# A fifth K pair with seven products in three gate/up chunks of each layer

## The chip, the core and the metric

The kernel runs on one core of a Trainium2 chip. Five engines work side by side, each with an instruction queue of its own: TensorE (PE, matmuls, with PEld for its weight loads), VectorE (DVE), ScalarE (ACT), GpSimd (POOL) and SyncE (SP, which here only issues DMAs). They wait for each other through semaphores. The metric is the device time of one execution in microseconds (us), the median of several.

## The reference

Two layers of a residual trunk over 256 tokens of width 2048, in float32. Each layer has a mixer (two kinds of attention, one input and one output projection) and a SwiGLU block. The change lies in the first half of the latter, the two products `h @ w_gate` and `h @ w_up`:

```python
def swiglu(h, w_gate, w_up, w_down):
    return (jax.nn.silu(h @ w_gate) * (h @ w_up)) @ w_down

for l in range(DEPTH):            # 2 layers
    ...
    h = rms_norm(x, pre_ffn_norm[l])
    f = swiglu(h, w_gate[l], w_up[l], w_down[l])
    x = x + rms_norm(f, post_ffn_norm[l])
```

`w_gate` and `w_up` are 2048 x 5632, `w_down` is 5632 x 2048.

## The kernel before

**Float32 products in three matmuls.** TensorE multiplies in a rounded format. Each operand is therefore split into a high part (ScalarE rounds it, `hi`, `xT[..., 0]`) and a low part (VectorE subtracts, `lo`, `xT[..., 1]`), and `product` (L1033) issues three matmuls: high by high, high by low, low by high (L1036, L1037, L1038). Weights come from memory as float32 tiles of 128 x 2 x 512, 512 KB each, one per K pair (2 x 128 rows of the weight matrix) and 512 columns. `weights_in_turn` holds them in the order in which they are used. `fetch` (L197) issues the loads, `feed` (L276) the splits, four tiles ahead of use (`LOOKAHEAD`).

**The gate/up loop.** The 5632 columns are cut into 11 chunks of 512 (c = 0 to 10), and for each chunk the loop at L1196 runs over 8 K pairs (kp = 0 to 7). A pair has four results to add to: gate and up, each for two halves of the tokens (`banks`, four PSUM banks). Plainly (`eight`, L1169) this takes 2 K halves x 2 token halves x 2 matrices = 8 products, 24 matmuls.

**Seven products.** For some pairs the kernel uses a Strassen-Winograd form (`seven`, L1179, and `seven_products`, L1053): the 2 x 2 blocks (token halves by K halves, and K halves by gate and up) are multiplied with 7 products, 21 matmuls. Four of these add to banks of their own (`extra`: p1, p6, p7, q5), which `shared_part` (L1070) combines once per chunk, after the last such pair. The form needs two more things:

- sums of the weights. `mixed_weights` (L243) makes them for each such pair. The up tile is not loaded alone: `summed` (L233) loads it into a tile `T` from SP's queue, and then POOL's queue (L238) adds the first half of the gate tile to it by an accumulating DMA. The gate tile goes to a tile `G` (L209). VectorE and ScalarE then split G (L286, L289) and T (L259, L260), form T's second half (L267) and G (L268) in place, and split these too (`Th`, `Tl`, L259, L260). There are 4 tiles T, 3 tiles G, 2 tiles each of Th and Tl, and 6 each of the high and low parts of all weights.
- sums of the activations, the `forms`. `pair_sums` (L1162) makes them once per layer and pair, with two sums f (L1166) and `token_sums` (L1040: four combinations, a high part on ScalarE, a low part at L1050). They are kept to the end of the loop, in four places (`sh`, `sl`). `FORM_AT` says before which chunk and position they are made.

Which pairs take seven products is laid down per chunk: pairs 4 and 6 in the first, 4, 5, 6 in the second, and 2, 4, 5, 6 (`SEVEN`) in all others. The other pairs are plain, and their tiles are loaded to `raw` (4 tiles).

**At the end of a chunk** VectorE adds the shared part to the banks and multiplies (L1220 to L1223), ScalarE applies SiLU, and TensorE transposes the result during the next chunk (`flip`). The next chunk adds up in the four banks that this one used as `extra`, and the other way round.

**Rooms.** `late_room` (L346) hands out places of 4 KB per partition, four in turn. In this stage they hold the residual x, which is written to memory in the fourth to seventh chunk (`put_away`), and from the eighth chunk on the activations.

**Order.** The kernel is written as one program. A scheduler orders each engine's queue when the kernel is built: by program order as priority, but by its own estimate of when an instruction can start, so that an instruction whose operands are late is passed by others, on TensorE too. Each queue is then fixed and runs in that order. `issue_after` ties an instruction behind another one: `behind` (L297) puts the next two plain low parts behind the shared part, `after_rests` (L304) puts a form behind the last plain low part, and `not_ahead` (L227) keeps loads of T and G behind a plain load six tiles earlier in the order.

Of the kernel before, what the change touches and what calls it, by code (L numbers as in the profile page):

```python
# [10 lines left out]
F32R = mybir.dt.float32r  # L11
# [6 lines left out]
P = 128  # L18
D = 2048
S = 256  # L20
# [22 lines left out]
SEVEN = (2, 4, 5, 6)  # L43
FIRST_SEVEN = (4, 6)
FIRST_ORDER = (0, 1, 3, 2, 7, 4, 6, 5)
NEXT_SEVEN = (4, 5, 6)
FORM_AT = {(0, 1): 4, (0, 2): 6, (0, 5): 5, (1, 3): 2}
DOWN_SEVEN = ((4, 7, 10, 12, 15, 17, 20), (3, 5, 8, 10, 13, 15, 18))

WARM = 10  # L50
# [10 lines left out]

def gate_sevens(c):

    return (FIRST_SEVEN, NEXT_SEVEN)[c] if c < 2 else SEVEN


# [87 lines left out]
def kernel(  # L154
# [191 lines left out]
    def late_room(shape, name, dtype=F32):  # L346

        return rooms.tile(shape, dtype, tag="late", name=name)
# [691 lines left out]
    def token_sums(pool, spool, bufs, a11, a12, a21, a22, nm, tags=("sh", "sl")):  # L1040

        s = pool.tile([P, 4, P], F32, tag="t2", name=f"s{nm}")
        nc.vector.tensor_tensor(out=s[:, 0, :], in0=a21, in1=a22, op=ALU.add)
        nc.vector.tensor_tensor(out=s[:, 1, :], in0=s[:, 0, :], in1=a11, op=ALU.subtract)
        nc.vector.tensor_tensor(out=s[:, 2, :], in0=a11, in1=a21, op=ALU.subtract)
        nc.vector.tensor_tensor(out=s[:, 3, :], in0=a12, in1=s[:, 1, :], op=ALU.subtract)
        sh = spool.tile([P, 4, P], F32R, tag=tags[0], bufs=bufs, name=f"sh{nm}")
        nc.scalar.activation(sh, s, AF.Copy)
        sl = spool.tile([P, 4, P], F32R, tag=tags[1], bufs=bufs, name=f"sl{nm}")
        nc.vector.tensor_tensor(out=sl, in0=s, in1=sh.bitcast(F32), op=ALU.subtract)  # L1050
        return [(sh[:, j, :], sl[:, j, :]) for j in range(4)]

# [30 lines left out]
    for l in range(L):  # L1083

        pool = Rooms(tc, f"att{l}")
# [12 lines left out]
        forms = {}  # L1098
        for n, (c, kp) in enumerate(plan[l]["order_o"][:16]):
# [5 lines left out]
            if n in (9, 11):  # L1105
                kp = O_SEVEN[(n - 9) // 2]
# [53 lines left out]
        forms = {}  # L1160

        def pair_sums(kp):  # L1162
            f = pool.tile([P, 2, S], F32, tag="t2", name=f"f{l}_{kp}")
            for kk in range(2):
                st = xT[2 * kp + kk]
                nc.vector.tensor_tensor(out=f[:, kk, :], in0=st[:, 0, :].bitcast(F32), in1=st[:, 1, :].bitcast(F32), op=ALU.add)  # L1166
            forms[kp] = token_sums(pool, gu, len(SEVEN), f[:, 0, 0:P], f[:, 1, 0:P], f[:, 0, P:S], f[:, 1, P:S], f"{l}_{kp}")

        def eight(banks, c, kp, toks, first, last):  # L1169
            g, u = weights(plan[l]["gate"][c, kp], LOOKAHEAD), weights(plan[l]["up"][c, kp], LOOKAHEAD)  # L1170
# [225 lines left out]
```

## Time and profile before

| | us |
|---|---|
| median of 3 runs | 2191.11 (2190.64 to 2191.31) |
| profiled execution, its own time | 2191.05 |
| its span, first to last instruction | 2189.4 |
| TensorE busy in the span | 2174.9 |
| VectorE busy | 1901.3 |
| ScalarE busy | 1370.9 |

The profile is of one execution. Its page gives the busy time of each engine, the chain of waits that ended last, and groups of instructions. In rows of instructions, `L289` is a line of the kernel, `lo<-raw,hi` says what is written and what is read, and the bracket at the end of a row in order of time says how long the engine had been idle and what ended that. Busy time of TensorE overlaps between successive matmuls, so distances between starts are used for it here. All times in rows are us from the start of the span, if no ns are given.

### The profile page before, as it was taken

What the parts mean: (1) busy time and instruction counts of PE and PEld (TensorE: products, weight loads), DVE (VectorE), ACT (ScalarE), POOL (GpSimd) and SP (SyncE); (2) the same over time, 40 slices, a digit from 0 to 9 for tenths busy, and PEclk for the clock granted to TensorE, in tenths of its full rate; (3) what the DMA queues carried; (4) which work ended last, traced back from release to release, by engine and by line L of the source; (5) the groups of instructions that cost most, each with busy time, mean ns of one, the idle gap of its engine ahead of it and who ended that gap; (6) DMA issues with size and microseconds to landing.
All of it is one profiled execution on the core that took longest, in us unless ns stands there. A gap on an engine that the chain in (4) does not pass through costs nothing.

```text
span 2189.4 us, 28540 instructions
## 1 busy us (share of the span) xinstructions
PE 2174.9 (99%) x9988; PEld 1791.1 (82%) x9988; DVE 1901.3 (87%) x2610; ACT 1370.9 (63%) x2051; POOL 139.1 (6%) x187
## 2 busy tenths in 40 slices
PE   9999999999999999999999999999999999999998
PEld 7888888888888888888878888888888888888886
DVE  6888658999999999989878886589999999999997
ACT  7666665756656656666665666657665666566664
POOL 1100000010010010000010000000000000100000
PEclk9999999999999999999999999999999999999999
DMA  9545555587687676767464555555867866767683
GB/s 327 189 164 173 192 184 172 180 281 231 219 272 229 198 258 203 247 211 260 147 241 173 177 177 185 193 168 194 277 208 255 256 210 228 238 214 233 207 266 100
DMA packets 138546, 467.28 MB, mean 213 GB/s; under 512 B 15761, under 2 KB 16785, under 8 KB 137889
## 3 DMA queue, kind: packets, MB, share of 16 engines
q1 hardware_dynamic: 122096, 436.29, 57.2%
q0 software_dynamic: 15872, 28.88, 7.5%
q8 instruction: 78, 1.28, 0.2%
q14 instruction: 68, 0.55, 0.1%
q10 hardware_dynamic: 432, 0.28, 0.0%
HBM read 457.00 MB, written 8.39 MB: 213 GB/s over the span
## 4 chain that ended last, share of the span: by engine, by line
PE 95%; DVE 3%; ACT 1%; DMA 0%; issue 0%; DVEq 0%; SPq 0%; ACTq 0%
PE c L1037 10%; PE c L1038 10%; PE c L1036 10%; PE in L1036 7%; PE in L1038 7%; PE in L1037 7%; PE dn L1280 4%; PE dn L1278 4%; PE dn L1277 4%; PE p L1037 3%; PE p L1038 2%; PE p L1036 2%; PE o L536 2%; PE o L537 2%; PE o L538 2%; PE dn L1037 1%
## 5 line engine op out<-in xcount | busy, mean ns | idle before, releaser
L289 DVE TENSOR_TENSOR lo<-raw,hi 128x1024 fp32r<-128x1024 f32 x522 | 625.4, 1219 | 97.6 <-ACT hi L286 96.6
L286 ACT ACTIVATE hi<-raw 128x1024 fp32r<-128x1024 f32 x522 | 540.6, 1055 | 186.0 <-issue 50.3
L1036 PE MATMUL c<-hi,xF 128*128 128x512 f32 x834 | 328.1, 394 | 0.1
L1037 PE MATMUL c<-lo,xF 128*128 128x512 f32 x834 | 325.1, 390 | 0.7 <-DVE lo L289 0.7
L1038 PE MATMUL c<-hi,xF 128*128 128x512 f32 x834 | 324.7, 390 | 0.0
L238 POOL DMA_DIRECT2D T<-in_weights_in_turn_dram x110 | 95.8, 871 | 1679.5 <-PE c L1037 521.3
L1037 PEld LDWEIGHTS c<-lo,xF 128*128 128x128 f32 x834 | 156.7, 188 | 33.4 <-DVE lo L289 2.5
L1038 PEld LDWEIGHTS c<-hi,xF 128*128 128x128 f32 x834 | 156.6, 188 | 32.7
L1036 PEld LDWEIGHTS c<-hi,xF 128*128 128x128 f32 x834 | 156.7, 188 | 31.4 <-ACT xF L455 0.5
L1277 PE MATMUL dn<-hi,jh 128*128 128x512 f32 x432 | 168.3, 389 | 0.0
L1278 PE MATMUL dn<-lo,jh 128*128 128x512 f32 x432 | 168.1, 389 | 0.0
L289 DVE TENSOR_TENSOR lo<-G,hi 128x1024 fp32r<-128x1024 f32 x110 | 134.1, 1219 | 29.7 <-ACT hi L286 29.7
L259 ACT ACTIVATE hi<-T 128x1024 fp32r<-128x1024 f32 x110 | 115.5, 1050 | 40.8 <-PE c L1038 26.5
L259 ACT ACTIVATE Th<-G 128x1024 fp32r<-128x1024 f32 x110 | 116.1, 1055 | 38.1 <-DVE G L268 36.2
L260 DVE TENSOR_TENSOR Tl<-G,Th 128x1024 fp32r<-128x1024 f32 x110 | 134.1, 1219 | 5.3 <-ACT Th L259 5.3
L260 DVE TENSOR_TENSOR lo<-T,hi 128x1024 fp32r<-128x1024 f32 x110 | 134.1, 1219 | 2.6 <-ACT hi L259 2.2
L268 DVE TENSOR_TENSOR G<-G,T 128x1024 f32<-128x1024 f32 x110 | 134.4, 1222 | 2.1
L259 ACT ACTIVATE Th<-T 128x512 fp32r<-128x512 f32 x110 | 68.9, 627 | 104.3 <-DVE T L267 88.3
L1280 PE MATMUL dn<-hi,jl 128*128 128x512 f32 x432 | 132.9, 390 | 0.0
L1036 PE MATMUL in<-hi,xT 128*128 128x512 f32 x328 | 131.9, 404 | 0.5 <-ACT hi L841 0.5
L1036 PE MATMUL in<-hi,xI 128*128 128x512 f32 x328 | 131.1, 401 | 0.0
L1038 PE MATMUL in<-hi,xT 128*128 128x512 f32 x328 | 128.4, 392 | 0.0
(450 smaller groups left out, 4735.6 us busy)
## 6 DMA issues: line engine op xcount, KB each, us to landing
raw<-in_weights_in_turn_dram SPq DMA_DIRECT2D x522, 512.0 KB, 4.6
T<-in_weights_in_turn_dram SPq DMA_DIRECT2D x110, 512.0 KB, 6.3
G<-in_weights_in_turn_dram SPq DMA_DIRECT2D x110, 512.0 KB, 5.8
T<-in_weights_in_turn_dram POOLq DMA_DIRECT2D x110, 256.0 KB, 7.1
GU<-in_weights_in_turn_dram SPq DMA_DIRECT2D x32, 512.0 KB, 6.2
V<-in_weights_in_turn_dram SPq DMA_DIRECT2D x8, 512.0 KB, 4.1
away_ffn<-x SPq DMA_DIRECT2D x8, 512.0 KB, 8.4
xd<-away_ffn SPq DMA_DIRECT2D x8, 512.0 KB, 8.2
```

What stands on the lines that cost most here:

```text
L238: nc.gpsimd.dma_start(sums[i][:, 0, :], stream[i - 1][:, 0, :], accum_op=ALU.add)
L259: nc.scalar.activation(h, w, AF.Copy)
L260: nc.vector.tensor_tensor(out=l, in0=w, in1=h.bitcast(F32), op=ALU.subtract)
L268: nc.vector.tensor_tensor(out=g, in0=g, in1=t2.unsqueeze(1).to_broadcast([P, 2, CW]), op=ALU.add)
L286: nc.scalar.activation(hi, raw, AF.Copy)
L289: rest = nc.vector.tensor_tensor(out=lo, in0=raw, in1=hi.bitcast(F32), op=ALU.subtract)
L1036: nc.tensor.matmul(a, sh, hi, start=first, stop=False, skip_group_check=open_sums[0])
L1037: nc.tensor.matmul(a, sh, lo, start=False, stop=False, skip_group_check=open_sums[0])
L1038: nc.tensor.matmul(a, sl, hi, start=False, stop=last, skip_group_check=open_sums[0])
L1277: nc.tensor.matmul(accs[c, t], sh, hi[:, kk, :], start=first, stop=False, skip_group_check=open_sums[0])
L1278: nc.tensor.matmul(accs[c, t], sh, lo[:, kk, :], start=False, stop=False, skip_group_check=open_sums[0])
L1280: nc.tensor.matmul(accs[c, t], sl, hi[:, kk, :], start=False, stop=last, skip_group_check=open_sums[0])
```

## The change

Pair 3 joins the pairs with seven products in chunks 5, 7 and 9, that is the sixth, eighth and tenth of each layer. Its form is made once per layer in chunk 4, before pair 3 there. The four places for forms are taken, so `token_sums` without a pool takes one late room, which has the size of both its tiles.

```diff
@@ -44,7 +44,9 @@
 NEXT_SEVEN = (4, 5, 6)
-FORM_AT = {(0, 1): 4, (0, 2): 6, (0, 5): 5, (1, 3): 2}
+MORE_SEVEN = (2, 3, 4, 5, 6)
+MORE_AT = (5, 7, 9)
+FORM_AT = {(0, 1): 4, (0, 2): 6, (0, 5): 5, (1, 3): 2, (4, 3): 3}
...
 def gate_sevens(c):
+    if c in MORE_AT:
+        return MORE_SEVEN
     return (FIRST_SEVEN, NEXT_SEVEN)[c] if c < 2 else SEVEN
...
@@ -1044,9 +1048,13 @@
-        sh = spool.tile([P, 4, P], F32R, tag=tags[0], bufs=bufs, name=f"sh{nm}")
+        if spool is None:
+            both = late_room([P, 2, 4, P], f"ss{nm}", F32R)
+            sh, sl = both[:, 0], both[:, 1]
+        else:
+            sh = spool.tile([P, 4, P], F32R, tag=tags[0], bufs=bufs, name=f"sh{nm}")
+            sl = spool.tile([P, 4, P], F32R, tag=tags[1], bufs=bufs, name=f"sl{nm}")
         nc.scalar.activation(sh, s, AF.Copy)
-        sl = spool.tile([P, 4, P], F32R, tag=tags[1], bufs=bufs, name=f"sl{nm}")
         nc.vector.tensor_tensor(out=sl, in0=s, in1=sh.bitcast(F32), op=ALU.subtract)
...
@@ -1164,7 +1172,7 @@
-            forms[kp] = token_sums(pool, gu, len(SEVEN), f[:, 0, 0:P], ...)
+            forms[kp] = token_sums(pool, gu if kp in SEVEN else None, len(SEVEN), f[:, 0, 0:P], ...)
```

More of the change, by code (lines that the diff above doesn't have):

```diff
@@ L1166, in pair_sums @@
                 nc.vector.tensor_tensor(out=f[:, kk, :], in0=st[:, 0, :].bitcast(F32), in1=st[:, 1, :].bitcast(F32), op=ALU.add)
-            forms[kp] = token_sums(pool, gu, len(SEVEN), f[:, 0, 0:P], f[:, 1, 0:P], f[:, 0, P:S], f[:, 1, P:S], f"{l}_{kp}")
+            forms[kp] = token_sums(pool, gu if kp in SEVEN else None, len(SEVEN), f[:, 0, 0:P], f[:, 1, 0:P], f[:, 0, P:S], f[:, 1, P:S], f"{l}_{kp}")
         def eight(banks, c, kp, toks, first, last):
```

## The prediction

> **What bounds the kernel now.** I read the page's busy times first, then the waits of TensorE, then busy times by chunk, then the order in time of TensorE and VectorE in one chunk.
>
> ```profile
> span 2189.4 us, 28540 instructions
> PE 2174.9 (99%) x9988; PEld 1791.1 (82%) x9988; DVE 1901.3 (87%) x2610; ACT 1370.9 (63%) x2051; POOL 139.1 (6%) x187
> ...
> PE p L1037 <- DVE Tl L260: 0.7, 2, 0.5
> ```
>
> TensorE is hardly ever idle: the longest entry for weights is 0.7 us in two waits (who waited; for what; us in all, times, longest). So time falls only if TensorE gets less to do, and rises if VectorE, busy 87% of the span, is late more often. The chunks from the fourth on are alike, so one window tells of them all:
>
> ```profile
> core 0: us, PE busy (x) PEld busy (x) DVE busy (x) ACT busy (x) POOL busy (x), PEclk, DMA share, GB/s
> 621.80:663.60 41.80, 41.80 (x190) 34.60 (x189) 38.99 (x42) 25.35 (x30) 3.46 (x4) 1.00 0.74 241
> ```
>
> The window runs from the start of pair 2 in the sixth chunk to that in the seventh. TensorE is full at full clock, VectorE has 2.8 us of air in 41.8, ScalarE 16. The order in time of TensorE in this window (start, duration, instruction):
>
> ```profile
> 621.84 0.39 PE L1036 MATMUL p<-hi,xF 128*128 128x512 f32 x1
> ...
> 626.60 0.39 PE L1036 MATMUL c<-hi,xF 128*128 128x512 f32 x1
> ...
> 632.04 0.39 PE L1036 MATMUL p<-hi,xF 128*128 128x512 f32 x1
> ...
> 641.56 0.39 PE L1036 MATMUL p<-hi,xF 128*128 128x512 f32 x1
> ...
> 643.83 0.39 PE L1037 MATMUL p<-Tl,sh 128*128 128x512 f32 x1
> ...
> 663.57 0.39 PE L1036 MATMUL p<-hi,xF 128*128 128x512 f32 x1
> ```
>
> Pair 2 with seven products takes 626.60 - 621.84 = 4.76 us for its 21 matmuls, 0.227 each; pair 3 with eight takes 632.04 - 626.60 = 5.44 for 24. A chunk takes 663.57 - 621.84 = 41.73, the window above unrounded.
>
> **The change part by part.** *What it removes.* In three chunks of each of two layers pair 3 goes from eight products to seven: three matmuls, 5.44 - 4.76 = 0.68 us, six times: **-4.08 us**. Transposes and products of other pairs stay.
>
> *What it adds on VectorE.* The kinds in one chunk (count | busy us, mean ns | idle before):
>
> ```profile
> L289 DVE TENSOR_TENSOR lo<-raw,hi 128x1024 fp32r<-128x1024 f32 x8 | 9.6, 1216 | 0.0
> L268 DVE TENSOR_TENSOR G<-G,T 128x1024 f32<-128x1024 f32 x4 | 4.9, 1222 | 0.1
> L289 DVE TENSOR_TENSOR lo<-G,hi 128x1024 fp32r<-128x1024 f32 x4 | 4.9, 1219 | 1.7 <-ACT hi L286 1.7
> L260 DVE TENSOR_TENSOR lo<-T,hi 128x1024 fp32r<-128x1024 f32 x4 | 4.9, 1217 | 0.0
> L260 DVE TENSOR_TENSOR Tl<-G,Th 128x1024 fp32r<-128x1024 f32 x4 | 4.9, 1217 | 0.0
> L267 DVE TENSOR_TENSOR T<-T 128x512 f32<-128x512 f32 x4 | 2.7, 685 | 0.0
> L260 DVE TENSOR_TENSOR Tl<-T,Th 128x512 fp32r<-128x512 f32 x4 | 2.7, 685 | 0.2 <-ACT Th L259 0.2
> L1074 DVE TENSOR_TENSOR w<-p,w 128x512 f32<-128x512 f32 x1 | 0.7, 692 | 0.6 <-PE p L1038 0.6
> ```
>
> A plain pair costs two low parts (L289). A mixed pair costs two low parts as well, and also T (L267), G (L268), and the low parts Tl of T and of G. Successive instructions overlap a little. The order in time of VectorE in the sixth chunk shows it:
>
> ```profile
> 619.53 1.22 DVE L260 TENSOR_TENSOR Tl<-G,Th 128x1024 fp32r<-128x1024 f32 x1
> 622.48 1.23 DVE L289 TENSOR_TENSOR lo<-G,hi 128x1024 fp32r<-128x1024 f32 x1 [1.73 <-ACT hi L286]
> ...
> 624.76 1.22 DVE L289 TENSOR_TENSOR lo<-G,hi 128x1024 fp32r<-128x1024 f32 x1
> ...
> 636.50 1.22 DVE L289 TENSOR_TENSOR lo<-raw,hi 128x1024 fp32r<-128x1024 f32 x1
> 637.64 0.68 DVE L267 TENSOR_TENSOR T<-T 128x512 f32<-128x512 f32 x1
> 638.24 1.22 DVE L289 TENSOR_TENSOR lo<-raw,hi 128x1024 fp32r<-128x1024 f32 x1
> ...
> 641.11 1.21 DVE L289 TENSOR_TENSOR lo<-raw,hi 128x1024 fp32r<-128x1024 f32 x1
> 642.25 1.21 DVE L260 TENSOR_TENSOR Tl<-G,Th 128x1024 fp32r<-128x1024 f32 x1
> ```
>
> The next start follows 1.14 us after that of a 128x1024 subtraction (637.64 - 636.50) and 0.60 after that of a 128x512 one (638.24 - 637.64). So a mixed pair costs 4 x 1.135 + 2 x 0.605 = 5.75 us against 2.27, **3.48 more**, and a changed chunk asks VectorE for 38.99 + 3.48 = 42.5 us while TensorE needs only 41.73 - 0.68 = 41.05. Two chunks together (changed, unchanged) ask 81.5 against 82.8: the debt can be paid, if one chunk may run late into the next.
>
> *Where the debt falls due.* The tightest place is Tl of pair 6: written until 642.25 + 1.21 = 643.46, read at 643.83. Its slack is 0.37 us. In the changed chunk the second half of pair 3's mixing, 3.48 us, comes ahead of this. It can begin when Tl of pair 2 is done (619.53 + 1.22), where VectorE now sits idle 1.73 us until a buffer of high parts comes free. That leaves 3.48 - 1.73 = 1.75 us of delay, and TensorE arrives 0.68 sooner: if all else keeps its order, Tl of pair 6 is 1.75 + 0.68 - 0.37 = **2.06 us late**. The other bound: three subtractions of plain weights (636.50, 638.24, 641.11; 1.13 each), needed only after pair 6, now go ahead of it. With all three behind it, it is 2.06 - 3.40 = 1.34 us early and nothing is lost. The scheduler puts them into gaps between dependent instructions, and their high parts come free as TensorE leaves pairs 4 and 5; I take it that two stay ahead by the new times and one (641.11) goes behind: 2.06 - 1.13 = 0.9 late, or 0.6 when I add up the work from 620.75: 3.48 + 3 x 5.75 + 2 x 1.13 = 23.0, ending 643.75 against 643.15.
>
> Lateness is not all lost, since TensorE's order is laid down with it. The second chunk shows how much. There the same three pairs 4, 5, 6 follow a form (below), and VectorE runs without a pause:
>
> ```profile
> 453.00:480.00 27.00, 26.51 (x117) 21.37 (x116) 26.96 (x34) 17.35 (x20) 1.73 (x2) 1.00 0.69 217
> ...
> 468.75 0.39 PE L1036 MATMUL p<-hi,xF 128*128 128x512 f32 x1
> ...
> 471.76 1.22 DVE L260 TENSOR_TENSOR Tl<-G,Th 128x1024 fp32r<-128x1024 f32 x1
> ...
> 472.16 0.39 PE L1038 MATMUL c<-hi,sl 128*128 128x512 f32 x1
> 473.04 0.50 PE L1037 MATMUL p<-Tl,sh 128*128 128x512 f32 x1 [0.49 <-DVE Tl L260]
> ```
>
> Pair 5 starts at 468.75, and by the order of the sixth chunk (643.83 - 641.56 = 2.27) its Tl would be due at 471.02. It ended at 472.98, 1.96 late. TensorE had taken another product first (472.16), and lost 473.04 - 472.16 - 0.23 = 0.65 us, a third. Of 0.6 to 0.9 late a third is 0.2 to 0.3; pair 5, one pair before, is squeezed too. I take **0.35 us lost in each run of five, 2.1 in all** (bounds 0 and 6 x 2.06 = 12.4).
>
> Behind the waiting matmul nothing but TensorE's own next products is queued. What is late next is the shared part (L1074): it now waits 0.6 us for TensorE, which covers some of the debt, and the next chunk's 1.73 us pause the rest, so the seventh, ninth and eleventh chunks cost nothing; without that cover each lost the remaining 1 us.
>
> *The form of pair 3.* Once per layer in the fifth chunk:
>
> ```profile
> L1166 DVE TENSOR_TENSOR f<-xF x16: 414/418/425, 418.5 to 1547.0; 128x256 f32<-128x256 f32 x16
> L1045 DVE TENSOR_TENSOR s<-f x8: 282/283/293, 419.2 to 1549.3; 128x128 f32<-128x128 f32 x8
> L1050 DVE TENSOR_TENSOR sl<-s,sh x36: 680/684/693, 423.2 to 2138.4; 128x512 fp32r<-128x512 f32 x36
> ```
>
> Two sums, four combinations and a low part (min/median/max ns): with the same overlap of 0.085, 2 x 0.33 + 4 x 0.20 + 0.60 = 2.06 us. The 1.73 us pause falls right behind the place where it is queued, and hides most of it; 0.33 is left against a slack of 0.37. Without that cover 2.06 - 0.37 = 1.7 us are late, and a third of it lost, 0.57. I take less than half of that, 0.25, **0.5 for two layers** (bounds 0 and 2 x 1.7 = 3.4). Its ScalarE copy and those of the mixing (two more per pair, L259) lie in ScalarE's 16 us of air.
>
> *Loads.* Pair 3's two loads become G and T of the same size, with an accumulating load from POOL of half the size on top, six times.
>
> ```profile
> 620.78 0.33 SPq L209 DMA_DIRECT2D G<-in_weights_in_turn_dram  x1
> ...
> T<-in_weights_in_turn_dram SPq DMA_DIRECT2D x110, 512.0 KB, 6.3
> G<-in_weights_in_turn_dram SPq DMA_DIRECT2D x110, 512.0 KB, 5.8
> T<-in_weights_in_turn_dram POOLq DMA_DIRECT2D x110, 256.0 KB, 7.1
> ...
> L286 ACT ACTIVATE hi<-G 128x1024 fp32r<-128x1024 f32 x110 | 115.7, 1052 | 12.0 <-PE c L1038 10.5
> ```
>
> T needs 6.3 + 7.1 = 13.4 us, but four T tiles let pairs 2 to 5 be loaded before the first of them is used, so I take 0. There are only three G tiles: G of pair 5 must wait until Tl of pair 2 is done, the very event that now lets the load at 620.78 go, and lands 5.8 later at 626.6. Its low part runs at 624.76 now and would at about 626.5; with 1.05 us for the high part it can start at 627.6. An order that has other work ready there hides this 1.1 us: cost 0, at most 1.1 per run. The form takes one of the four rooms of x that were put away one chunk earlier, and the later chunks' rooms move on by one, each free long before: 0.
>
> **Sum**, against the profiled execution's own 2191.05 (span 2189.4 and 1.65 around it; the median of the three runs is 0.06 higher): 2191.05 - 4.08 + 2.1 + 0.5 = **2189.6**, -0.07%.
>
> **The rivals.** *All hidden* (2187.0): the order puts all three plain subtractions behind and the form in the pause. For it: 81.5 against 82.8 us for two chunks, and the pause of 1.73. Against it: the 0.37 slack, and the second chunk's loss.
>
> *The order stays* (2200.5, slower): in place Tl of pair 6, the scheduler goes on filling gaps with plain weights as at 636.50 to 641.11, and TensorE stands 2.06 us in each run: 6 x (2.06 - 0.68) = +8.3, and 2 x 0.57 for the form. It decides against the change from 0.68 us a run on, and beyond 0.2% from 1.4. For it: that order in each chunk. Against it: the product taken first at 472.16.
>
> *Three G tiles* (2190.9 to 2197.7, say 2194.3): VectorE idles 1.1 us for pair 5's gate weights, Tl of pair 6 is 0.6 + 1.1 = 1.7 late; with a third of it lost 0.57 a run, with all lost 1.7; and 0.5 for the form. Against it: plain work and T of pair 5 can go first.
>
> *Each changed chunk takes VectorE's time* (2195.5 to 2200.3): if no debt passes to the next chunk, a chunk lasts 42.47, or 43.27 with the 0.6 and 0.2 of idle time that its dependences force (L1074, Tl of T), instead of 41.73: 0.74 to 1.54, six times. Against it: two sets of accumulators let the next chunk's products start before the evacuation ends. The Trainium skill, Perfetto Trace Analysis, "Identifying the Most-Contended Engine", says that for Vector the occupancy is a fair measure of how close it is to its limit and that the engine with the highest occupancy is the one to relieve. By that rule the change loads the wrong engine. The trace agrees that VectorE is near its limit (38.99 of 41.80), not that it sets the time so far.
>
> **How the numbers follow.** The forecast has 0.50, all hidden 0.25, three G tiles 0.10, the order stays 0.09, VectorE's time 0.04, unnamed 0.02. A measurement here can tell about 0.2% from no change, 4.4 us: 2186.7 and 2195.5 are the bounds. All hidden lies 0.3 within the lower bound: a fourth of its chance goes beyond, 0.07 faster with rounding. Slower: 0.09 + 0.04 + 0.03 of three G tiles = 0.16. The rest, 0.77, is the same. The range leaves out these ends: 2186.8 to 2195.0. The forecast's own, with 0 to 0.68 lost a run and 0 to 0.57 a form, is 2187.0 to 2192.2.
>
> **What would show it.** Eighteen matmuls fewer; in the changed chunks a wait of TensorE for Tl (L260) of pair 5 or 6, 0.2 to 0.5 us in all; no idle time of VectorE before pair 4's low part; 41.73 us as before for the unchanged chunks behind them. A wait for Tl over 1.4 us a run, VectorE idle for `hi` of pair 5 behind a G load, or a longer seventh, ninth or eleventh chunk would prove the forecast wrong, and so would time that moves in other stages.

## The result and the profile after

The changed kernel takes 2193.82 us (median of 21 executions, 2192.34 to 2196.9) against 2191.4 of the kernel before (21 executions beside it, 2189.78 to 2192.61): 1.0013 times as long, 95% interval 1.0007 to 1.0019. It is 2.4 us slower. That is less than the 0.2% that was called no change, but the forecast of 2189.6 lay 1.5 us on the faster side. The profiled execution took 2192.96 us.

From the page of the changed kernel, its span, its busy times and the longest entry for weights among TensorE's waits:

```profile
span 2191.3 us, 28616 instructions
...
PE 2175.0 (99%) x9970; PEld 1784.5 (81%) x9970; DVE 1923.6 (88%) x2648; ACT 1380.1 (63%) x2065; POOL 144.4 (7%) x193
...
PE p L1041 <- DVE Tl L264: 1.7, 4, 0.5
```

The eighteen matmuls are gone (9988 to 9970), yet TensorE is busy 2175.0 us as before (2174.9). Its waits for Tl grew by only 1.0 us, from 0.7 to 1.7. So most of what was lost isn't in rows of waits; it shows in the distances between starts. (Lines of the kernel moved by 4 to 8: L1036 to L1038 of before are L1040 to L1042, L260 is L264, L289 is L293, L1074 is L1082.)

The same chunk as in the prediction, first layer, TensorE's starts of pair 2 and pair 6 of the sixth chunk and of pair 2 of the seventh:

```profile
620.96 0.40 PE L1040 MATMUL p<-hi,xF 128*128 128x512 f32 x1
...
640.33 0.39 PE L1040 MATMUL p<-hi,xF 128*128 128x512 f32 x1
...
662.49 0.39 PE L1040 MATMUL p<-hi,xF 128*128 128x512 f32 x1
```

From pair 2 to pair 6 it is 19.37 us, before 641.56 - 621.84 = 19.72; from pair 6 to the next pair 2 it is 22.16, before 22.01. Taken for every chunk, these two distances tell where the time went. Differences to the kernel before, in us, for the first layer and the second:

| from | to | first | second |
|---|---|---|---|
| fifth, pair 6 (the form is made) | sixth, pair 2 | +0.48 | +0.45 |
| sixth, pair 2 | pair 6 (eight to seven products: -0.68) | -0.35 | -0.35 |
| sixth, pair 6 | seventh, pair 2 | +0.15 | +0.12 |
| seventh, pair 2 | pair 6 | +0.25 | +0.23 |
| seventh, pair 6 | eighth, pair 2 | +0.05 | +0.04 |
| eighth, pair 2 | pair 6 (-0.68) | -0.50 | -0.48 |
| eighth, pair 6 | ninth, pair 2 | +0.09 | +0.04 |
| ninth, pair 6 | tenth, pair 2 | +0.66 | +0.66 |
| tenth, pair 2 | pair 6 (-0.68) | -0.64 | -0.66 |
| tenth, pair 6 | eleventh, pair 2 | +0.69 | +0.64 |
| eleventh, pair 6 | down stage | +0.16 | +0.17 |
| fifth, pair 2 | down stage | **+1.03** | **+0.82** |

What is not listed moved by at most 0.02. The two layers agree within 0.05, as one expects of fixed queues. The sum is +1.85 of the 1.9 us between the two spans. Outside the stretch the two executions differ too, by parts that happen to cancel: the first layer enters it 1.36 us sooner, and between the two stretches 1.41 us are lost. In the kernels below, e8 and e12 left aside, the rest of the span differs from the kernel before by -1.2 to +2.0 us, with and without the change.

A step that starts at pair 6 holds pair 6's own products, and the starts of the single matmuls show that nearly all that such a step loses is lost there (0.65 of the ninth chunk's 0.66 and 0.68 of the tenth's 0.69 in the first 22 matmuls). So the table divides into three:

- **In the changed chunks** 0.68 us was to be saved each time. At pair 5, ahead of pair 6, 0.33, 0.18 and 0.04 of it are lost in the first layer, and at pair 6 another 0.15, 0.09 and 0.69. With the second layer this is 2.8 us.
- **In the chunks behind them**, whose own work did not change, 0.30, 0.66 and 0.16 are lost in the first layer, 2.2 us in both.
- **The form** costs 0.9 us.

Together this is 5.9 us against 4.08 saved.

VectorE by chunk, from pair 2 to pair 2, for the fifth, sixth, seventh and ninth chunk (columns as in the prediction):

```profile
core 0: us, PE busy (x) PEld busy (x) DVE busy (x) ACT busy (x) POOL busy (x), PEclk, DMA share, GB/s
578.75:620.96 42.21, 42.09 (x190) 34.49 (x189) 41.11 (x50) 25.81 (x31) 3.23 (x4) 1.00 0.74 227
620.96:662.49 41.53, 41.53 (x186) 33.80 (x185) 40.56 (x45) 26.10 (x31) 4.35 (x5) 1.00 0.75 239
662.49:704.52 42.03, 42.03 (x189) 34.42 (x188) 40.83 (x45) 26.13 (x31) 4.03 (x5) 1.00 0.79 241
...
745.84:788.24 42.40, 42.05 (x189) 34.49 (x188) 41.04 (x45) 25.69 (x31) 3.96 (x5) 1.00 0.72 219
```

VectorE goes from 38.99 us a chunk to between 40.56 and 41.11 in these. In the sixth and seventh together it works 81.39 of 83.56 us, with 2.17 left. The granted clock (PEclk) is 1.00 in all four.

VectorE in the sixth chunk, the counterpart of the prediction's rows:

```profile
619.51 1.23 DVE L264 TENSOR_TENSOR Tl<-G,Th 128x1024 fp32r<-128x1024 f32 x1
620.65 0.68 DVE L271 TENSOR_TENSOR T<-T 128x512 f32<-128x512 f32 x1
621.61 1.23 DVE L293 TENSOR_TENSOR lo<-G,hi 128x1024 fp32r<-128x1024 f32 x1 [0.27 <-ACT hi L290]
...
638.86 1.21 DVE L293 TENSOR_TENSOR lo<-raw,hi 128x1024 fp32r<-128x1024 f32 x1
...
641.73 1.21 DVE L293 TENSOR_TENSOR lo<-raw,hi 128x1024 fp32r<-128x1024 f32 x1
642.87 1.21 DVE L264 TENSOR_TENSOR Tl<-G,Th 128x1024 fp32r<-128x1024 f32 x1
644.00 2.35 DVE L293 TENSOR_TENSOR lo<-raw,hi 128x1024 fp32r<-128x1024 f32 x2
```

This is the order that the prediction counted on: the pause is down from 1.73 to 0.27, two plain low parts stand ahead of pair 6's Tl, the third behind. Tl is done at 644.08 (forecast 643.75). But TensorE starts pair 2 at 620.96, not at 621.84 as in the kernel before, while VectorE's Tl of pair 2 stands where it stood (619.51, before 619.53). So VectorE enters this chunk with 1.45 us of lead in place of 2.31. TensorE around pair 6:

```profile
638.00 0.39 PE L1042 MATMUL p<-Th,sl 128*128 128x512 f32 x1
638.38 0.50 PE L1041 MATMUL p<-Tl,sh 128*128 128x512 f32 x1
638.72 0.40 PE L1042 MATMUL p<-Th,sl 128*128 128x512 f32 x1
...
642.82 0.49 PE L1040 MATMUL p<-Th,sh 128*128 128x512 f32 x1
643.15 0.40 PE L1042 MATMUL p<-Th,sl 128*128 128x512 f32 x1
...
644.55 0.40 PE L1041 MATMUL p<-Tl,sh 128*128 128x512 f32 x1
```

By the order of before, pair 6's Tl would be due at 640.33 + 2.27 = 642.60, so it is 1.48 us late (forecast 0.6 to 0.9). TensorE takes other products, reads it at 644.55 and loses 0.15. More is lost at pair 5: steps of 0.38 and 0.34 us (638.00 to 638.72) in place of 0.227 each.

The tenth chunk, also changed, keeps the order of the kernel before: all three plain low parts (the first at 804.94) stay ahead of pair 6's Tl.

```profile
806.68 1.22 DVE L293 TENSOR_TENSOR lo<-raw,hi 128x1024 fp32r<-128x1024 f32 x1
...
809.55 1.22 DVE L293 TENSOR_TENSOR lo<-raw,hi 128x1024 fp32r<-128x1024 f32 x1
810.68 1.22 DVE L264 TENSOR_TENSOR Tl<-G,Th 128x1024 fp32r<-128x1024 f32 x1
```

```profile
807.32 0.39 PE L1040 MATMUL p<-hi,xF 128*128 128x512 f32 x1
...
809.36 0.39 PE L1040 MATMUL p<-Th,sh 128*128 128x512 f32 x1
809.69 0.50 PE L1041 MATMUL p<-Tl,sh 128*128 128x512 f32 x1
810.17 0.50 PE L1040 MATMUL p<-Th,sh 128*128 128x512 f32 x1
...
811.96 0.50 PE L1041 MATMUL p<-Tl,sh 128*128 128x512 f32 x1
```

Tl is done at 811.90, due at 807.32 + 2.27 = 809.59: 2.31 late, of which 0.69 is lost. In the eighth it is 0.80 late, with two plain low parts ahead, and 0.09 is lost at pair 6.

Now the seventh chunk, which has no fifth pair. VectorE, ScalarE and TensorE at its pair 2:

```profile
661.25 0.68 DVE L264 TENSOR_TENSOR Tl<-T,Th 128x512 fp32r<-128x512 f32 x1
663.14 1.23 DVE L293 TENSOR_TENSOR lo<-G,hi 128x1024 fp32r<-128x1024 f32 x1 [1.21 <-ACT hi L290]
664.28 1.22 DVE L264 TENSOR_TENSOR Tl<-G,Th 128x1024 fp32r<-128x1024 f32 x1
```

```profile
662.04 1.06 ACT L290 ACTIVATE hi<-G 128x1024 fp32r<-128x1024 f32 x1
663.01 1.04 ACT L263 ACTIVATE Th<-G 128x1024 fp32r<-128x1024 f32 x1
```

```profile
665.22 0.39 PE L1042 MATMUL p<-Th,sl 128*128 128x512 f32 x1
665.55 0.50 PE L1041 MATMUL p<-Tl,sh 128*128 128x512 f32 x1
```

Before, Tl of pair 2 was done when the pause began (619.53 + 1.22, then 1.73 idle). Here VectorE comes late, the pause of 1.21 us stands *ahead* of that Tl, and so does the low part of pair 4 for which VectorE waited: ScalarE makes that high part first (662.04) and Th of pair 2 after it. Tl ends at 665.50, and TensorE's step before it takes 0.33 (665.22 to 665.55). The idle time did not pay the debt; it fell where it cost 0.25 us.

The ninth chunk, also unchanged, at pair 6:

```profile
765.94 1.22 DVE L293 TENSOR_TENSOR lo<-raw,hi 128x1024 fp32r<-128x1024 f32 x1
767.07 1.21 DVE L264 TENSOR_TENSOR Tl<-G,Th 128x1024 fp32r<-128x1024 f32 x1
```

```profile
767.61 0.39 PE L1040 MATMUL p<-Th,sh 128*128 128x512 f32 x1
768.34 0.50 PE L1041 MATMUL p<-Tl,sh 128*128 128x512 f32 x1 [0.35 <-DVE Tl L264]
```

This Tl needs no more work than before and ends at 768.28, but TensorE, ahead by what the eighth chunk saved, would have read it at 767.84. The slack of 0.37 us is overdrawn by 0.44, and here all of it is lost, the step taking 0.73 us (767.61 to 768.34).

### The profile page after: what moved, and what is told of

It is laid out like the page before. It is cut to its first block, busy times and chain, and to the rows that moved or that the text cites. A ratio compares the mean times of both kernels' runs of the same rounds, so it can differ in the third digit from the quotient of the medians.

```text
span 2191.3 us, 28616 instructions
## 1 busy us (share of the span) xinstructions
PE 2175.0 (99%) x9970; PEld 1784.5 (81%) x9970; DVE 1923.6 (88%) x2648; ACT 1380.1 (63%) x2065; POOL 144.4 (7%) x193
## 4 chain that ended last, share of the span: by engine, by line
PE 88%; DVE 7%; issue 2%; ACT 1%; DMA 1%; DVEq 0%; SPq 0%; ACTq 0%
PE c L1041 8%; PE c L1040 8%; PE c L1042 8%; PE in L1040 7%; PE in L1042 7%; PE in L1041 7%; PE dn L1288 4%; PE dn L1285 4%; PE dn L1286 4%; PE p L1041 2%; PE p L1042 2%; PE p L1040 2%; PE o L540 2%; PE o L541 2%; PE o L542 2%
## 5 line engine op out<-in xcount | busy, mean ns | idle before, releaser
L293 DVE TENSOR_TENSOR lo<-raw,hi 128x1024 fp32r<-128x1024 f32 x510 | 610.8, 1218 | 97.7 <-ACT hi L290 96.4
L290 ACT ACTIVATE hi<-raw 128x1024 fp32r<-128x1024 f32 x510 | 527.6, 1055 | 188.5 <-DMA raw<-in_weights_in_turn_dram 62.3
L1040 PE MATMUL c<-hi,xF 128*128 128x512 f32 x792 | 311.8, 394 | 0.1
L1041 PE MATMUL c<-lo,xF 128*128 128x512 f32 x792 | 308.9, 390 | 1.0 <-DVE lo L293 1.0
L1042 PE MATMUL c<-hi,xF 128*128 128x512 f32 x792 | 308.4, 390 | 0.0
L1041 PEld LDWEIGHTS c<-lo,xF 128*128 128x128 f32 x792 | 148.8, 188 | 32.4 <-DVE lo L293 3.2
L1042 PEld LDWEIGHTS c<-hi,xF 128*128 128x128 f32 x792 | 148.7, 188 | 31.2
L1040 PEld LDWEIGHTS c<-hi,xF 128*128 128x128 f32 x792 | 148.8, 188 | 29.8 <-ACT xF L459 0.5
L290 ACT ACTIVATE hi<-G 128x1024 fp32r<-128x1024 f32 x116 | 122.2, 1053 | 56.1 <-PE c L1042 37.4
L293 DVE TENSOR_TENSOR lo<-G,hi 128x1024 fp32r<-128x1024 f32 x116 | 141.3, 1218 | 12.7 <-ACT hi L290 12.7
L264 DVE TENSOR_TENSOR Tl<-G,Th 128x1024 fp32r<-128x1024 f32 x116 | 141.3, 1218 | 8.5 <-ACT Th L263 8.2
L264 DVE TENSOR_TENSOR lo<-T,hi 128x1024 fp32r<-128x1024 f32 x116 | 141.2, 1217 | 3.3 <-ACT hi L263 2.9
L1040 PE MATMUL in<-hi,xT 128*128 128x512 f32 x328 | 131.4, 402 | 0.4 <-ACT hi L845 0.4
L1040 PE MATMUL in<-hi,xI 128*128 128x512 f32 x328 | 131.1, 401 | 0.0
L1041 PE MATMUL in<-lo,xI 128*128 128x512 f32 x328 | 128.0, 390 | 0.3 <-DVE lo L293 0.3
```

What stands on the lines that cost most here:

```text
L264: nc.vector.tensor_tensor(out=l, in0=w, in1=h.bitcast(F32), op=ALU.subtract)
L290: nc.scalar.activation(hi, raw, AF.Copy)
L293: rest = nc.vector.tensor_tensor(out=lo, in0=raw, in1=hi.bitcast(F32), op=ALU.subtract)
L1040: nc.tensor.matmul(a, sh, hi, start=first, stop=False, skip_group_check=open_sums[0])
L1041: nc.tensor.matmul(a, sh, lo, start=False, stop=False, skip_group_check=open_sums[0])
L1042: nc.tensor.matmul(a, sl, hi, start=False, stop=last, skip_group_check=open_sums[0])
```

## The experiments

Where an experiment is told by places, the differences to the kernel before are summed for a layer over four stretches: the form (fifth chunk's pair 2 to the sixth's), sixth and seventh chunk, eighth and ninth, tenth to the down stage.

| us a layer, first / second | form | sixth, seventh | eighth, ninth | tenth to down | sum |
|---|---|---|---|---|---|
| the change | +.48 / +.44 | +.10 / +.05 | +.25 / +.21 | +.20 / +.13 | +1.03 / +0.82 |
| e1 form alone | +.45 / +.42 | +.03 / -.03 | +.03 / -.03 | +.01 / -.03 | +0.51 / +0.33 |
| e2 no form | +.01 / .00 | +.14 / -.02 | +.10 / +.63 | +.28 / +.73 | +0.53 / +1.35 |
| e3 fewer products | +.02 / .00 | -.65 / -.68 | -.65 / -.68 | -.67 / -.68 | -1.96 / -2.04 |
| e5 3.0 us relieved | +.45 / +.44 | -.65 / -.71 | -.65 / -.71 | -.67 / -.71 | -1.53 / -1.68 |
| e13 1.2 us, pairs 2, 3 | +.43 / +.44 | -.10 / -.61 | -.65 / -.36 | -.46 / -.64 | -0.78 / -1.17 |
| e14 1.2 us, pairs 5, 6 | +.43 / +.44 | -.50 / -.14 | -.25 / -.37 | -.60 / -.27 | -0.93 / -0.34 |
| e9 tied | +.49 / +.48 | +2.19 / +2.13 | +.16 / +.14 | +.18 / +.11 | +3.02 / +2.86 |
| e10 sixth and tenth only | +.43 / +.44 | +.08 / +.09 | +.10 / .00 | +.31 / +.22 | +0.92 / +0.74 |

### The parts of the change alone

**e1, the form without the fifth pair.**

```diff
-MORE_AT = (5, 7, 9)
+MORE_AT = ()
```

> The form of pair 3 is made in the fifth chunk, but no chunk uses it; all chunks keep their products of before. Debt theory (VectorE's added work is the cost): the form costs 0.48 us per layer, all of it at pair 6 of the fifth chunk (the step from pair 6 there to pair 2 of the sixth chunk is 22.49 us instead of 22.01), every later step as before: +1.0 us, some 2192.3. Rival (the form hides in the pause of 1.73 us, and that wait comes from the first run of five): 22.01 us, +0.0.

2192.27 us against 2190.97, ratio 1.0003 (0.9994 to 1.0013). By places, the form costs 0.45 and 0.42 us, all of it at one step, from pair 6 of the fifth chunk to the sixth. That is nearly twice the 0.25 of the forecast. The pause at the start of the sixth chunk shows what the form takes besides:

```profile
621.07 1.22 DVE L264 TENSOR_TENSOR Tl<-G,Th 128x1024 fp32r<-128x1024 f32 x1
623.16 1.23 DVE L293 TENSOR_TENSOR lo<-G,hi 128x1024 fp32r<-128x1024 f32 x1 [0.87 <-ACT hi L290]
```

It lasts 0.87 us in place of 1.73: the form alone uses half of the pause that the first run of five was to use.

**e2, the fifth pair without its form.**

```diff
-FORM_AT = {..., (1, 3): 2, (4, 3): 3}
+FORM_AT = {..., (1, 3): 2}
-            seven_products(banks, extra, forms[kp], ...)
+            seven_products(banks, extra, forms[kp if kp in forms else 2], ...)
```

> Pair 3 takes seven products in the three chunks, but with the form of pair 2, so that no form is made and the output is not the reference's. Debt theory: the fifth chunk is as before, the runs still lose 0.85 us each against 0.68 gained: +0.2 per run, about +0.9 us in all, some 2192.3. Rival (the form is what spoils it, the runs are covered): -4.08 us, 2187.3. If the loads of G are late (three G tiles): VectorE idles over 1 us ahead of pair 5's low part in each run.

2192.9 us, ratio 1.0007 (0.9998 to 1.0017). By places, the runs of five alone give back all that they save, +0.53 and +1.35 us a layer, so the loss is there without the form. The two do not simply add up: both layers together stand at +1.88 without the form and at +1.85 with it. Without it VectorE enters the sixth chunk with its full lead, but all three plain low parts then stay ahead of pair 6's Tl in every changed chunk. This Tl is 2.1 to 2.3 us late by the order of before, and 0.55 to 0.72 is lost from pair 6 on.

**e3, the kernel before with one product of pair 3 left out in the same chunks.**

```diff
+                        if c in (5, 7, 9) and (kp, kk, t, col) == (3, 1, 1, 1):
+                            continue
                         product(banks[2 * t + col], stat, ...)
```

> The kernel before, with one of the eight products of pair 3 left out in the sixth, eighth and tenth chunks: TensorE gets the change's 0.68 us less, VectorE nothing more. Debt theory: the slack of 0.37 us at pair 6 is overdrawn by 0.31, of which a third is lost: -4.08 + 6 x 0.1 = -3.5 us, 2187.9. Rival (TensorE's saving cannot be had at all, since VectorE already sets the pace of a chunk through the buffers): about 0. Rival (all of it can be had): -4.08.

2187.96 us, ratio 0.9983 (0.9974 to 0.9992). Each chunk keeps 0.65 to 0.68 us and nothing is lost behind it: TensorE's being early by itself costs nothing here, not even the 0.1 us a run that was expected from the slack of 0.37. The loss is made by what the change adds beside that.

### The amount of VectorE's work, or its order

**e5, the second half of T not formed in the mixed pairs of the changed chunks.**

```diff
-        nc.vector.tensor_tensor(out=t2, in0=t2, in1=u[:, 0, :], op=ALU.subtract)
+        if i not in lighter:
+            nc.vector.tensor_tensor(out=t2, in0=t2, in1=u[:, 0, :], op=ALU.subtract)
```

Here `lighter` holds the up tiles of pairs 2 to 6 in the sixth, eighth and tenth chunks.

> The changed kernel, in which the second half of T is not formed in the five mixed pairs of the three changed chunks (one subtraction of 0.605 us of VectorE less per pair, 3.0 per chunk, against the 3.48 that the change adds); the output is not the reference's. If the amount of VectorE's work is the cause: nothing is lost in the runs, the stretch from pair 2 to pair 6 takes 19.04 us and that from pair 6 to the next pair 2 22.0 in all chunks but the fifth (form, 22.46): -2.04 + 0.45 per layer, -3.2 us against before. If loads, G tiles or the number of products kept in flight are the cause: as the changed kernel, +2.4.

2186.7 us in one execution, before 2191.14 (13 executions, none below 2190.04). The form's cost stays; the loss of the runs is gone, each changed chunk keeps what it kept in e3. Its sixth and seventh chunk by windows:

```profile
core 0: us, PE busy (x) PEld busy (x) DVE busy (x) ACT busy (x) POOL busy (x), PEclk, DMA share, GB/s
...
620.48:661.54 41.06, 41.06 (x187) 34.01 (x185) 38.56 (x41) 26.25 (x31) 4.37 (x5) 1.00 0.80 246
661.54:703.29 41.75, 41.75 (x190) 34.58 (x188) 39.85 (x43) 25.86 (x31) 4.37 (x5) 1.00 0.77 237
```

The loads, the G tiles, ScalarE's copies and the products are those of the changed kernel. With 78.41 us of work for VectorE in 82.81 nothing is lost; in the changed kernel, with 81.39 in 83.56, these two chunks lose 0.78. So it is the mixing on VectorE that takes back what TensorE saves. But the left-out subtraction is also a step of the chain that leads to Tl, and the order changes with it: pair 6's Tl of the sixth chunk has one plain low part ahead of it in place of two and ends 0.62 us before pair 6 starts (first layer). The amount of work, the length of that chain and the order are not told apart by this run.

**e13 and e14, the same for two pairs only**, `lighter` with pairs 2 and 3, and with pairs 5 and 6.

> The changed kernel, but the second half of T is not formed in pairs 2 and 3 of the changed chunks, so the sums of the weights are wrong there: 2 x 0.60 = 1.2 us less for VectorE per changed chunk, against 3.0 when it was left out in all five pairs. Theory (total work): the sixth and seventh chunk ask 81.4 - 1.2 = 80.2 us, and with the 2.2 us that VectorE stood idle there 82.4, within TensorE's 82.8: at least 0.55 of the 0.68 us is kept in each run, so a layer is at about -1.2 to -1.6 us with its 0.45 for the form. Rival (the loss falls in proportion): 1.2 of 3.0 us bring back 0.4 of the 0.83 lost, 0.33 a run, so a layer is at -0.1 us. Second rival (place): work taken away early is used up by the idle time before pair 4's low part and brings nothing, +0.8 to +1.0.

> The same 1.2 us taken away at the tight place: the second half of T is not formed in pairs 5 and 6 of the changed chunks, so their sums of the weights are wrong. Theory (total work): the same as with pairs 2 and 3, within 0.3 us a layer. Rival (place): Tl of pair 6 is done 1.2 us earlier for certain, so the step from pair 2 to pair 6 and that behind it keep all of the 0.68 us in each changed chunk, and a layer is at least 0.6 us below the kernel relieved in pairs 2 and 3.

The medians, 2191.43 and 2190.55 us against 2191.29, have intervals of some 0.1% to either side (ratios 1.0, 0.9989 to 1.0012, and 0.9999, 0.9988 to 1.001) and cannot tell these apart. By places, a run loses 0.21 us on average of six with pairs 2 and 3 relieved and 0.32 with pairs 5 and 6 (0.68 less what is kept), against 0.84. So 1.2 us of 3.0 bring back about two thirds of the loss, more than in proportion, though the theory's 0.55 us kept was missed by both (0.47 and 0.36). A single run loses between 0.03 and 0.58, and the two layers of one execution differ by up to 0.6 us in sum, so these averages are rough; "within 0.3 us a layer" holds for the first layer (0.15) and not for the second (0.83). The rival of place falls: relief at the tight place was not 0.6 us better, it was no better at all. And relief in pairs 2 and 3 leaves the chains of pairs 5 and 6 as they are, so their length is not the whole cause.

**e4, every plain low part of a chunk tied behind the last Tl**, second to tenth chunk; the tie is put into `feed`.

```diff
-            with behind():
+            with behind() if held[1] or mixed_low[0] is None or i + 1 in sevens else tc.issue_after(mixed_low[0].ins):
                 rest = nc.vector.tensor_tensor(out=lo, ...)
```

> The changed kernel; from the second to the tenth chunk, plain low parts are queued on VectorE behind the last low part of the mixed pair ahead of them, so that two to three of 1.13 us no longer stand before Tl of pair 6. If order is the cause: the waits for Tl at pair 6 vanish in the changed chunks and in the eighth and ninth, about 0.5 us per run, 3 us in all: 2190.8, and the second chunk loses less. If only the amount of VectorE's work counts: 2193.8, and the wait turns up at the start of the next chunk, behind the shared part.

2210.73 us, ratio 1.009 (1.0072 to 1.0108): a miss for both. The plain tiles are given back later, which presumably starts their loads later. ScalarE's group of plain high parts:

```profile
L292 ACT ACTIVATE hi<-raw 128x1024 fp32r<-128x1024 f32 x510 | 527.1, 1055 | 257.9 <-DMA raw<-in_weights_in_turn_dram 165.1 <-PE in L1045 21.4 <-PE c L1045 17.1
```

It waits 165.1 us for loads, 62.3 in the changed kernel and 41.8 in the kernel before. The order was not tested by this, a new wait was made.

**e9, the same tie on pair 7's two low parts alone, in the changed chunks alone.**

```diff
-            with behind():
+            with tc.issue_after(last_low[0].ins) if i in tied else behind():
                 rest = nc.vector.tensor_tensor(out=lo, ...)
```

> The changed kernel, but in the sixth, eighth and tenth chunks the two low parts of pair 7's plain weights wait until the last Tl of pair 6 is done; the rest as it is. Theory (VectorE has too much work in a changed chunk, wherever it stands): the step from pair 2 to pair 6 gets the 0.3 us back that the sixth chunk loses there, but pair 7 or the next mixed pairs are late by as much, so from the fifth chunk's pair 2 to the down stage a layer stays within 0.4 us of the changed kernel (+0.8 to +1.0 against before). Rival (the order decides): the plain low parts that stood ahead were the loss; each changed chunk keeps its 0.68 us, the steps after pair 6 cost nothing more, a layer is at -1.5 us and the time at 2188.5. A miss for both would be a longer wait for pair 7's own low parts, over 0.5 us a chunk.

2199.31 us, ratio 1.0037 (1.0023 to 1.0052). The eighth to eleventh chunks lose within 0.1 us of what they lose without the tie, at other places; the sixth and seventh lose 2.1 us more. The rival, that the plain low parts ahead of Tl were the loss, falls; of the theory, "within 0.4 us" was a miss. VectorE in the sixth chunk shows what the low parts had been doing ahead of Tl:

```profile
641.11 0.69 DVE L264 TENSOR_TENSOR Tl<-T,Th 128x512 fp32r<-128x512 f32 x1
642.88 1.22 DVE L264 TENSOR_TENSOR Tl<-G,Th 128x1024 fp32r<-128x1024 f32 x1 [1.09 <-ACT Th L263]
644.03 4.62 DVE L293 TENSOR_TENSOR lo<-raw,hi 128x1024 fp32r<-128x1024 f32 x4
```

They filled the 1.09 us in which ScalarE makes Th. Without them VectorE stands idle. Pair 6's Tl begins 21.73 us after the start of pair 2 (642.88 - 621.15), with them 21.91 (642.87 - 620.96), and four low parts are left for later.

**e10, the fifth pair in the sixth and tenth chunks only.**

```diff
-MORE_AT = (5, 7, 9)
+MORE_AT = (5, 9)
```

> The changed kernel with pair 3 in the sixth and tenth chunks alone, so that three chunks without it lie between the runs of five. Theory (VectorE's lead is used up and one unchanged chunk does not restore it): the ninth chunk no longer stalls at pair 6 (+0.66 us in the changed kernel, 0 here), and the tenth chunk with the rest behind it loses less than it saves: at most +0.4 us after its pair 6 in place of +0.69 and +0.16, so a layer is at +0.2 to +0.4 us. Rival (each run of five pays for itself, whatever went ahead): the tenth chunk loses as before, -0.64 and then +0.69 and +0.16, and a layer is at +0.45 for the form, +0.1 for the sixth chunk and +0.2 for the tenth, +0.75 us.

2193.59 us, ratio 1.001 (1.0001 to 1.002). Each theory has one part right. The ninth chunk's stall is gone (+0.07 and +0.02 in place of +0.66), so that was the eighth chunk's debt. But the tenth chunk loses as before, -0.57 and then +0.76 at its own pair 6 in the first layer, though three chunks of the old kind went ahead: each of the two runs of five loses about what it saves within two chunks.

**e6, pair 1 in place of pair 3.**

```diff
-MORE_SEVEN = (2, 3, 4, 5, 6)
-FORM_AT = {..., (4, 3): 3}
+MORE_SEVEN = (1, 2, 4, 5, 6)
+FORM_AT = {..., (4, 3): 1}
```

> The changed kernel with pair 1 instead of pair 3 as the fifth: pairs 1, 2, 4, 5, 6, so a plain pair stands between. VectorE's work per chunk is the same. Amount theory: the same 0.85 us is lost per run, wherever it shows, +2.4 us against before. Rival (five in a row are the trouble: the last of the row is late): the row is three long as before, the runs lose less than 0.3 us each: -4.08 + 1.8 + 0.9 for the form, -1.4 us.

2191.43 us in one execution, before 2191.14. By places the two layers are at -0.28 and -0.31, each some 1.2 us better than with pair 3. If the form costs as much here as in e1, 0.43 us a run are lost. So the amount theory (0.85 wherever it shows) and the rival (under 0.3) were both missed: the same work for VectorE costs about half where plain pair 3 stands between the mixed ones, and its place in the chunk matters that much. The gain of 0.6 us by places is below what one execution can show.

### Can POOL take the work?

**e7, the form's sums and combinations on POOL**, and **e8, T's second half there too.**

```diff
-        nc.vector.tensor_tensor(out=s[:, 0, :], in0=a21, in1=a22, op=ALU.add)
+        eng = nc.vector if spool is not None else nc.gpsimd
+        eng.tensor_tensor(out=s[:, 0, :], in0=a21, in1=a22, op=ALU.add)
...
-        nc.vector.tensor_tensor(out=t2, in0=t2, in1=u[:, 0, :], op=ALU.subtract)
+        (nc.gpsimd if on_pool[0] else nc.vector).tensor_tensor(out=t2, in0=t2, in1=u[:, 0, :], op=ALU.subtract)
```

The last two lines are e8's alone, second to tenth chunk. In both kernels the form is no longer tied behind the plain low parts.

> The changed kernel; the two sums and four combinations of pair 3's form are made on POOL, VectorE keeps the low part (0.60 us). Form theory: the step from pair 6 of the fifth chunk to pair 2 of the sixth goes back from 22.48 to 22.0, the rest stays: 0.9 us less than the changed kernel, +1.5 against before. Rival (VectorE and POOL hold each other up): no gain, 22.4 or more.

> As e7_form_pool, and the second half of T is formed on POOL in the second to tenth chunks: 0.605 us of VectorE's work less for each mixed pair, 2.4 to 3.0 per chunk. Amount theory: the runs lose nothing, -4.08 against before and the second chunk's 0.87 less per layer, -4 to -5.5. Rival (the chain becomes longer: a 128x128 operation on POOL takes 0.46 us beside an idle VectorE and up to 1.5 beside a busy one, against 0.60 for 128x512 on VectorE): Tl of pair 6 is later still, slower than the changed kernel, +3 or more.

2195.22 us, ratio 1.0021 (1.0011 to 1.0031; one of ten executions took 7812 us), and 2261.61, ratio 1.0321 (1.0306 to 1.0336). The rivals came true. The form on POOL costs +0.55 and +1.69 us in place of +0.48 and +0.44. T's second half takes 1.91 us there, VectorE waits 103.6 us for it in all, and TensorE waits for Tl over and over:

```profile
PE p L1042 <- DVE Tl L264: 35.9, 21, 3.3
```

**e11, pair 7's two plain low parts on POOL** in the fifth and the changed chunks, off the chain from T to Tl; and **e12**, pair 3 in six chunks (`MORE_AT = (5, 6, 7, 8, 9, 10)`) with three plain low parts of each on POOL.

```diff
+            if i in on_pool:
+                nc.gpsimd.tensor_tensor(out=lo, in0=raw, in1=hi.bitcast(F32), op=ALU.subtract)
+                ready[i] = (hi, lo)
+                fed[0] += 1
+                continue
             with behind():
                 rest = nc.vector.tensor_tensor(out=lo, ...)
```

> The changed kernel with pair 7's two plain low parts on POOL in the fifth, sixth, eighth and tenth chunks, so VectorE has 2.27 us less to do in each of them, just where it is late. A half-size operation took POOL 1.9 us when T was formed there, so a low part should take 3.8, two 7.6, and they have about 10 us until pair 7 is due. Theory (the amount of VectorE's work is the loss): the fifth chunk's step after pair 6 loses at most 0.2 us in place of 0.45, and a changed chunk with the one behind it keeps at least 0.5 of its 0.68 us: -1.3 to -1.9 us a layer between the fifth chunk's pair 2 and the down stage, 2187.5 to 2188.6 in all. Rival (POOL is too slow or its loads come late): TensorE waits for the low parts of pair 7, or the accumulating loads behind them on POOL's queue bring T late, over 0.7 us a changed chunk, and the time is above 2192.

> Pair 3 with seven products in each of the sixth to eleventh chunks, with three plain low parts of each of them on POOL (pair 7's two and pair 0's up; in the fifth chunk pair 7's two): 3.40 us less for VectorE against 3.48 more. Twelve runs of five would save 8.2 us if nothing were lost. Theory (amount): each keeps at least 0.45 us, so 5.4 to 8.2 are saved and 0 to 0.5 a layer is lost to the form: 2183 to 2186.5, faster than both kernels. Rival (POOL late): POOL needs 11.4 us for the low parts and 3.5 for its loads in a chunk of 41, but pair 0's low part and the accumulating loads queue behind each other; TensorE waits over 0.7 us a chunk and the time is above 2191.

2232.66 us, ratio 1.0189 (1.0175 to 1.0203), and 2285.61, ratio 1.0428 (1.0413 to 1.0442). The times are those of the rivals, but not for the reason that they gave. POOL and VectorE in e11's fifth chunk:

```profile
592.32 5.54 POOL L293 TENSOR_TENSOR lo<-raw,hi 128x1024 fp32r<-128x1024 f32 x2 [2.51 <-ACT hi L290]
```

```profile
592.74 2.90 DVE L264 TENSOR_TENSOR Tl<-T,Th 128x512 fp32r<-128x512 f32 x1
595.56 3.38 DVE L264 TENSOR_TENSOR lo<-T,hi 128x1024 fp32r<-128x1024 f32 x1
598.87 1.21 DVE L264 TENSOR_TENSOR Tl<-G,Th 128x1024 fp32r<-128x1024 f32 x1
```

POOL is quicker than expected (2.77 us each here, 2.97 on average, not 3.8), but while it works VectorE hardly does: two instructions that cost 0.68 and 1.22 elsewhere take 2.90 and 3.38. From 592.74 to 598.87, 6.13 us, VectorE does 0.60 + 1.135 = 1.74 us of work by the distances of the prediction. Two low parts taken over save it 2.27 us and cost it 4.4, and TensorE's waits for Tl come to 28.7 us, up to 3.8 at once. The Trainium skill, SBUF — State Buffer, "Who interferes with whom", says that a VectorE instruction with two inputs in SBUF contends with a GpSimd instruction that reads SBUF. The trace agrees, with these 6.13 us for 1.74.

The waits are not the whole price. Behind the first of them in this chunk, a step of 4.15 us, seven steps of TensorE take 0.43 us in place of 0.227, and the granted clock of that stretch is 0.83:

```profile
600.00:610.00 10.00, 9.87 (x36) 8.00 (x37) 7.78 (x10) 5.45 (x6) 1.76 (x2) 0.83 1.03 331
```

No version that was tried and leaves no work out beats both kernels by more than a measurement resolves.

## Why the prediction was wrong

**The products, -4.08: right.** e3 keeps 0.65 to 0.68 us six times, with nothing lost.

**VectorE's 3.48 us more: right. The order: right in four of six.** In the sixth and eighth chunk the pause was filled, two plain low parts stayed ahead and one went behind, and TensorE took other products first. In the tenth all three stayed ahead.

**0.35 us lost in each run: too little.** In the changed chunks 0.47 us a run were lost, 2.8 in all in place of 2.1. Pair 6's Tl was 1.48, 0.80 and 2.31 us late in the first layer, not 0.6 to 0.9. For the sixth chunk one reason is on record: the 1.73 us pause at its start was spent twice, once to hide the form and once for pair 3's mixing. The form alone takes it down to 0.87 (e1). "A third" is no fixed share either: 0.15 of 1.48, 0.09 of 0.80 and 0.69 of 2.31 were lost, and in the ninth chunk all of 0.44.

**"The next chunk's 1.73 us pause the rest, so the seventh, ninth and eleventh chunks cost nothing": this step failed.** These chunks lost 0.30, 0.66 and 0.16 us in the first layer and 0.27, 0.66 and 0.17 in the second, 2.2 us for a forecast of 0. Where VectorE came late the pause stood ahead of the low part that TensorE needed next (seventh chunk), or TensorE stood waiting for a low part that came 0.44 us after it was due (ninth). With what was lost in the changed chunks that makes 0.84 a run (six runs: 1.85 - 0.92 + 4.08 = 5.0), more than the 0.68 saved. Of the 3.4 us between forecast and profiled execution, 2.2 are this step, 0.7 the runs and 0.4 the form. The prediction had the price, "without that cover each lost the remaining 1 us", and did not give it a chance. It added 81.5 us of work against 82.8 of TensorE's time and took the 1.3 us between them as free for the debt. In the sixth and seventh chunk 2.17 us were left over all the same, 1.5 of them in waits for ScalarE's high parts, which stand at their places in fixed queues. How much of the idle time can be used was not measured by itself.

**What is shown of the cause and what is not.** TensorE's saving costs nothing by itself (e3), and the loss vanishes when 3.0 of the 3.48 us of mixing are taken from VectorE again (e5); so the mixing on VectorE makes it. That the amount alone decides is not shown: with the same amount a run loses about half as much when pair 1 is the fifth (e6), and in e5 and e14 the chain to pair 6's Tl is shorter too. e13, where it is not, speaks for the amount. Why the pause moved ahead of pair 2's Tl in the seventh chunk is read from ScalarE's order there, and no kernel was made that changes this alone.

**The form, 0.25 each: mis-sized.** It costs 0.48 and 0.44 us, alone nearly as much (e1). The bound without cover was 0.57.

**The loads, 0: right.** Pair 5's gate weights have their low part at 627.36 without a wait of VectorE ahead of it, so the rival of three G tiles did not occur. The 0.27 us stand before pair 4's low part and are what is left of the pause.

**The rivals.** "The order stays" came true in the tenth chunk as to the order, but not as to the price: 0.69 us were lost there, not 2.06. "Each changed chunk takes VectorE's time" named the engine that decided, but not the size. The changed chunks lasted 41.53 us in the sixth, not 42.47: the debt was paid at pairs 5 and 6 and in the next chunk. The Trainium skill (Perfetto Trace Analysis, "Identifying the Most-Contended Engine") tells to optimize the engine with the highest occupancy first. In the changed kernel, relieving VectorE (e5) took the stretch from +1.85 to -3.21; but in the kernel before, TensorE alone relieved (e3) gained 4.0 us there with VectorE's work unchanged.

**The sum, by what was measured**: 2191.05 - 4.08 + 5.0 for the runs + 0.9 for the form is 2192.9, against 2192.96 of the profiled execution. That it closes so well is luck in part, since what differs outside the stretch cancels.

## What to carry to other kernels

When an engine gets more work than a stage can hold, add up its work *and* the idle time that its dependences force on it over the stages that are to share the debt; idle time in a profile is spare only if other work is ready for it at that place. A cover that the sum leans on (here the pause) can be spent only once and needs its own check: what stands in the queue before and after it once the engine comes late, and a rival with its price. Small instructions that seem to be in the way may be what fills a dependent chain's gaps, and an idle engine is no place for work if it shares a path with the one to be relieved.

## What the runs showed of the hardware

A 128x1024 subtraction on POOL takes 2.77 us (e11, in the rows shown) and holds VectorE's subtractions back for nearly as long: two of them made 1.74 us of VectorE's work last 6.13 (e11). A late operand costs TensorE more than its wait: around one, distances between matmuls are 0.33 to 0.38 us in place of 0.227, while the rows show a busy engine (638.00 to 638.72). So the waits left out four fifths of this loss: those for Tl grew by 1.0 us, the runs and the form lost 5.9. Behind a long wait the matmuls were slower for a while: seven steps of 0.43 us behind a step of 4.15, at a granted clock of 0.83 (e11).
